# Sample states of the two recurrences in six half buffers instead of three whole ones

## The chip, the cores and the metric

The kernel runs on one core of one Trainium2 chip. The metric is device time in microseconds, from one launch of the whole program. Its engines are named as in the profile: PE is TensorE's matmul, PEld its weight load, DVE is VectorE, ACT is ScalarE, POOL is GpSimd, SP is SyncE; SPq is the queue on which SyncE issues DMAs.

## The reference, cut to what matters

The reference is one step of a hybrid decoder layer for a prompt (512 tokens) and eight samples (8 tokens each) that share all weights. The layer projects the input once, runs a Mamba-2 recurrence (SSD) and an mLSTM recurrence beside each other, projects back, and follows with cross attention and a SwiGLU block. Each sample brings a state for each recurrence, and the new states are outputs. For a group of samples the two recurrences compute:

```python
# SSD, per head: h is 64 x 128 (16 heads)
y_inter = einsum('btgn,bgjpn->btgjp', cc, h) * exp(cum)[..., None]
h_new = h * exp(cum[:, -1])[..., None, None] + einsum('bsgj,bsgjp,bsgn->bgjpn', to_end, xc, bc)
# mLSTM, per head: C is 128 x 256 (4 heads), n is 128
num = einsum('btsh,bshv->bthv', s, vc) + s_inter[..., None] * einsum('bthd,bhdv->bthv', qc, c_st)
c_new = scale[..., None, None] * c_st + einsum('bsh,bshd,bshv->bhdv', w_end, kc, vc)
```

So each sample's state is read once by a matmul (what the tokens see of the old state), scaled by a decay, increased by an outer product of the sample's own tokens, and stored.

## The kernel before, in words

Everything is computed in 32-bit floats. Large weights are split in a high and a low part, so that a projection is three matmuls per block (L201, L202, L203 for most, L772 to L774 for the values); these fill TensorE nearly all the time. The program's instructions are put in order ahead of time by a planner that simulates the engines: an instruction that stands earlier in the program has precedence as soon as its inputs are there by the planner's clock, and later ones fill the gaps. The result is one fixed order for each engine and for each DMA queue; on the chip every engine takes its list in that order and waits where an input is late.

The change is in two stages, both of which run among projection matmuls.

**SSD of the samples** (pool `ssds`, from L651). `xdts` (tokens times step size) and `xes` (`xdts` times the decay to the end) are tiles of 64 x 16 x 64. `stacks` (L637) builds from them, once for each half batch `hb`, the two operands of the update in a 96-row form (copies on ACT at L643, L644, L646, L648, differences on DVE at L645, L647). Then a loop over `b` from 0 to 3 handles two samples at a time, `4 * hb + b` for `hb` 0 and 1. Each sample's state is a tile `h0` of 128 x 16 x 64 (512 KB), which the profile calls h. In a step:

- L711 loads the two states on SyncE's queue.
- L715 reads them: four matmuls, one for each group of eight heads `g` and half batch `hb`, each with a stationary of 32 columns and 512 moving columns. They accumulate over the steps in four strips of 32 rows of one PSUM tile `psh` (ps_hs in the profile). The profile shows each of these 32-bit matmuls as two records. Their order is given by L712 and L713:

```python
        for g in range(2):
            for hb in (1, 0):
```

- L721 masks the sample's tokens (ACT), L722 multiplies the whole state by its decay (POOL), L725 computes the outer product of a head group (`ps_hu`), L726 adds it on DVE, and L728 stores the whole state after the second group.

`xdts`, `xes` and the states share one tag, `t4`, with three buffers: the first two hold `xdts` and `xes` until their readers are done, and a later load waits until the state that was in its buffer has been stored. `psh` holds one of the two PSUM buffers of its pool during the loop, so `ps_hu` has the other.

**mLSTM of the samples** (pool `mls`, from L870). For each half batch, four samples follow each other. Each state `c0` (128 x 4 x 258, 516 KB, c in the profile) is loaded by L909, read by four matmuls at L911, one for each head, into four strips of `psn` (ps_nh), updated head by head by L918 (`ps_cu`) and L919 (one DVE instruction for decay and sum), and stored by L921. Here too the tag is `t4` with three buffers, in a pool of its own.

Of the kernel before, what the change touches and what calls it, by code (L numbers as in the profile page):

```python
# [11 lines left out]
F32 = mybir.dt.float32  # L12
F32R = mybir.dt.float32r
BF16 = mybir.dt.bfloat16
AF = mybir.ActivationFunctionType
ALU = mybir.AluOpType
# [3 lines left out]
P = 128  # L20
T = 576
TP = 512
TS = 64
# [93 lines left out]
def build(nc, tc, ctx, I, O):  # L117
    V, A, G, S, TE = nc.vector, nc.scalar, nc.gpsimd, nc.sync, nc.tensor
    mm = TE.matmul
# [22 lines left out]
    def BP(name="b"):  # L142
        return pb.tile([P, 512], F32, name=name, tag="b")
# [140 lines left out]
    wend = ml.tile([P, 5, 16], F32, name="wend")  # L284
# [20 lines left out]
    for k in range(KT):  # L305
        if k % 2 == 0:
            c = slice(128 * k, 128 * k + 256)
            S.dma_start(raws[0][:, c], I["win"][1][:, c])
        S.dma_start(xraw[:, k, :], I["xT"][:, k, :])
        if k % 2 == 0:  # L310
# [4 lines left out]
                                     op0=ALU.mult, op1=ALU.subtract)  # L315
# [27 lines left out]
    stop = gemm(ps0[2][1], [(*w2, KT)], U, UL, 256, 320, 0, NSS)  # L343
# [12 lines left out]
    stop = gemm(ps0[3][0], [(*w3, KT)], U, UL, 0, 256)  # L356
# [19 lines left out]
    vts = ml.tile([P, 4, 258], F32, name="vts")  # L376
    ghalf = ml.tile([P, KT], F32, name="ghalf")
    V.tensor_scalar(ghalf, PAR("g_ml"), 0.5, None, op0=ALU.mult)
    stb = ExitStack()
# [257 lines left out]
    def stacks(pool, a, b, hb, nb=1):  # L637

        r, o = slice(32 * hb, 32 * hb + 32), slice(32 - 32 * hb, 64 - 32 * hb)
        l = slice(64, 96)  # L640
        sa_ = pool.tile([96, a.shape[-1]], F32R, name="sta", tag="sta", bufs=nb)
        sb_ = pool.tile([96, b.shape[-1]], F32R, name="stb", tag="stb", bufs=nb)
        A.copy(sa_[r, :], a[r, :])  # L643
        A.copy(sa_[o, :], a[r, :])  # L644
        V.tensor_tensor(sa_[l, :], a[r, :], sa_[r, :].bitcast(F32), op=ALU.subtract)  # L645
        A.copy(sb_[r, :], b[r, :])  # L646
        V.tensor_tensor(sb_[o, :], b[r, :], sb_[r, :].bitcast(F32), op=ALU.subtract)  # L647
        A.copy(sb_[l, :], b[r, :])  # L648
        return sa_, sb_

    st2 = ExitStack()  # L651
    sd = st2.enter_context(tc.tile_pool(name="ssds", bufs=1, side="right", reuse_waits="tile"))
    masks8 = C16("masks")[:TS, :].unsqueeze(1).to_broadcast([TS, 8, TS])
    xdts = sd.tile([TS, 16, 64], F32, name="xdts", tag="t4", bufs=3)
    xes = sd.tile([TS, 16, 64], F32, name="xes", tag="t4", bufs=3)
    btk = sd.tile([TS, 2, P], F32, name="btk")
    for g in range(2):
        ps = BP("ps_xts")
        for j in range(4):
            TE.transpose(ps[:TS, j * P:(j + 1) * P], xs[:, g * 4 + j, TP:T], ident)  # L660
        V.tensor_tensor(xdts[:, 8 * g:8 * g + 8, :], ps[:TS, :].rearrange("p (h k) -> p h k", h=8),
                        CT[:TS, 4, 32 + 8 * g:40 + 8 * g].unsqueeze(2).to_broadcast([TS, 8, 64]), op=ALU.mult)
    ps = BP("ps_bts")
    for g in range(2):
        TE.transpose(ps[:TS, g * P:(g + 1) * P], bc[:, g, TP:T], ident)
    A.copy(btk, ps[:TS, 0:256].rearrange("p (g k) -> p g k", g=2))
    G.tensor_tensor(xes, xdts, wend[:TS, 4, :].unsqueeze(2).to_broadcast([TS, 16, 64]), op=ALU.mult)

    cpad = sd.tile([P, 2, NB, 32], F32, name="cpad")
    G.memset(cpad, 0.0)  # L670
# [8 lines left out]
    for g in range(2):  # L679
        psb = BP("ps_ls")  # L680
        pb3 = psb.rearrange("p (h t) -> p h t", h=8)
        for h in range(8):
            mm(psb[:, h * TS:(h + 1) * TS], sel[:80, 8 * g + h:8 * g + h + 1].to_broadcast([80, P]), cumst[:, TP:T],
               start=h == 0, stop=h == 7, skip_group_check=True)
        A.activation(decs[:, 8 * g:8 * g + 8, :], pb3[:, :, 7:TS:8], AF.Exp)
        lm = sd.tile([TS, 8, TS], F32, name="lms", tag="ts", bufs=1)
        V.tensor_tensor(lm, pb3[:TS], CT[:TS, 4, 8 * g:8 * g + 8].unsqueeze(2).to_broadcast([TS, 8, TS]), op=ALU.subtract)
        G.tensor_tensor(lm, lm, masks8, op=ALU.add)
        A.activation(lm, lm, AF.Exp)
        pcb = BP("ps_cbs")  # L690
        mm(pcb[:TS, :TS], bc[:, g, TP:T], bc[:, 2 + g, TP:T], start=True, stop=True)
        V.tensor_tensor(lm, lm, pcb[:TS, :TS].unsqueeze(1).to_broadcast([TS, 8, TS]), op=ALU.mult)
        for h in range(8):
            k, j = h % 2, (8 * g + h) // 2
            mm(psi[64 * k:64 * k + 64, j * TS:(j + 1) * TS], xdts[:, 8 * g + h, :], lm[:, h, :], start=True, stop=True,
               skip_group_check=True)
    yds = sd.tile([P, 8, TS], F32, name="yds", tag="ts", bufs=1)
    G.tensor_tensor(yds, xs[:, :, TP:T], PAR("dskip").unsqueeze(2).to_broadcast([P, 8, TS]), op=ALU.mult)
# [5 lines left out]
    A.activation(ecg[0:64, :], ps[0:64, 0:8], AF.Exp)  # L704
    A.activation(ecg[64:128, :], ps[64:128, 8:16], AF.Exp)
    psh = BP("ps_hs")
    hbs = [stacks(sd, btk.rearrange("p g k -> p (g k)"), xes.rearrange("p h k -> p (h k)"), hb, 2) for hb in range(2)]
    for b in range(4):
        hns = [sd.tile([P, 16, 64], F32, name="h0", tag="t4", bufs=3) for _ in range(2)]
        for hb in range(2):  # L710
            S.dma_start(hns[hb], I["h0"][4 * hb + b])  # L711
        for g in range(2):  # L712
            for hb in (1, 0):  # L713
                q = 32 * (2 * g + hb)
                mm(psh[q:q + 32, :], cpad[:, g, 4 * hb + b, :],  # L715
                   hns[hb][:, 8 * g:8 * g + 8, :].rearrange("p h k -> p (h k)"),
                   start=b == 0, stop=b == 3, skip_group_check=True)
        for hb in range(2):
            bb, hn, (bst, xst) = 4 * hb + b, hns[hb], hbs[hb]
            bm = sd.tile([96, 256], F32R, name="bm", tag="bm", bufs=1)  # L720
            A.activation(bm, bst.bitcast(F32), AF.Copy, scale=C32("bmask")[:96, b:b + 1])  # L721
            G.tensor_tensor(hn, hn, decs[:, :, bb:bb + 1].to_broadcast([P, 16, 64]), op=ALU.mult)  # L722
            for g in range(2):
                ps = BP("ps_hu")
                mm(ps, bm[:, g * P:(g + 1) * P], xst[:, g * 512:(g + 1) * 512], start=True, stop=True)  # L725
                V.tensor_tensor(hn[:, 8 * g:8 * g + 8, :], hn[:, 8 * g:8 * g + 8, :],  # L726
                                ps.rearrange("p (h k) -> p h k", h=8), op=ALU.add)
            S.dma_start(O["ssms"][bb], hn.rearrange("p h k -> p (h k)"))  # L728
    yin = sd.tile([P, 8, 64], F32, name="yin", tag="ts", bufs=1)
    V.tensor_tensor(yin, psh.rearrange("p (h k) -> p h k", h=8), ecg.unsqueeze(2).to_broadcast([P, 8, 64]), op=ALU.mult)  # L730
    ps = BP("ps_yt")
# [166 lines left out]
                    wendm[:TS, 4, :].unsqueeze(2).to_broadcast([TS, 4, P]), op=ALU.mult)  # L898
    for hb in range(2):
        r = slice(32 * hb, 32 * hb + 32)  # L900
        kst, vst = stacks(ms, kws.rearrange("p h k -> p (h k)"), vts.rearrange("p h k -> p (h k)"), hb)
        psn = BP("ps_nh")
        for h in range(4):
            mm(psn[32 * h:32 * h + 32, 0:257], ds_[r, h, r], vt[4][r, h, 0:257], start=True, stop=False,
               tile_position=(32 * hb, 32 * h), skip_group_check=True)
        for b in range(4):
            bb = 4 * hb + b
            c0 = ms.tile([P, 4, 258], F32, name="c0", tag="t4", bufs=3)
            S.dma_start(c0, I["c0"][bb])  # L909
            for h in range(4):  # L910
                mm(psn[32 * h:32 * h + 32, 0:257], qpad[:, h, bb, :], c0[:, h, 0:257], start=False, stop=b == 3,  # L911
                   skip_group_check=True)
            km = ms.tile([96, 512], F32R, name="km", tag="km", bufs=1)
            A.activation(km, kst.bitcast(F32), AF.Copy, scale=C32("bmask")[:96, b:b + 1])
            cn = c0
            for h in range(4):
                ps = BP("ps_cu")
                mm(ps[:, 0:258], km[:, h * P:(h + 1) * P], vst[:, h * 258:(h + 1) * 258], start=True, stop=True)  # L918
                V.scalar_tensor_tensor(cn[:, h, :], c0[:, h, :], es[:, h, 8 * bb + 7:8 * bb + 8], ps[:, 0:258],  # L919
                                       op0=ALU.mult, op1=ALU.add)  # L920
            S.dma_start(O["cs"][bb], cn)  # L921
        num = ms.tile([P, 1, 257], F32, name="nums", tag="nums", bufs=1)
        V.tensor_copy(num[:, 0, :], psn[:, 0:257])
        m4 = ms.tile([4, 4, 32], F32, name="m4t", tag="m4t", bufs=1)
        V.tensor_tensor(m4, C32("m4")[:4, :].rearrange("p (h t) -> p h t", h=4),
                        mrow[:, r].unsqueeze(1).to_broadcast([4, 4, 32]), op=ALU.mult)
        psx = BP("ps_mx")
        mm(psx[:, 0:1], m4.rearrange("p h t -> p (h t)"), ones[:4, :], start=True, stop=True)
        ex = ms.tile([P, 1], F32, name="exs", tag="exs", bufs=2)
        A.activation(ex, psx[:, 0:1], AF.Exp, scale=-1.0)  # L930
        f = head_norm(num, ex, 1, ms, "s")
        hn = ms.tile([P, 256], F32, name="hns", tag="hns", bufs=1)
        V.tensor_scalar(hn, num[:, 0, 0:256], f, None, op0=ALU.mult)
        pst = BP("ps_hts")
        for dv in range(2):
            TE.transpose(pst[:, dv * P:(dv + 1) * P], hn[:, dv * P:(dv + 1) * P], ident)
        A.copy(qk[:, :, TP + 32 * hb:TP + 32 * hb + 32], pst[:, 0:256].rearrange("p (d t) -> p d t", d=8))
# [1474 lines left out]
```

## Time and profile before

| what | value |
|---|---|
| median of the runs shown | 1121.05 us (1120.54 to 1121.95) |
| the profiled execution | 1117.7 us |
| its span, first to last instruction | 1115.9 us |
| mean granted TensorE clock over the span | 0.996 |
| PE busy | 1095.6 us (98%) |
| DVE, ACT, POOL busy | 771.4, 609.8, 223.5 us |
| matmuls L715 into psh | from 141.7 to 207 us |
| updates L726 of the SSD states | from 146.7 to 216.5 us |
| mLSTM states, first load to last store issued | from 260.5 to 390.2 us |

The profile is of one execution. In the rows of the timeline the first number is the start in us from the span's start, the second how long the row lasts, then come the engine, the line of the kernel, the operation, output<-inputs, the shape (for PE the stationary and then the moving operand) and how many records are merged into the row. A bracket at the end gives idle time of the engine just before, and what ended it. In a row of SPq the time is that of issuing the DMA, not of its transfer. In groups of instructions the columns are busy us and mean ns of one, then idle time before them. DMA issues give the size of one and the median us from issue to landing.

### The profile page before, as it was taken

How to read it: one execution, taken by the hardware profiler on the slowest of the kernel's cores; microseconds unless marked ns; L12 is line 12 of the kernel's file. 1: busy time of each engine (PE TensorE's matmuls, PEld its weight loads, DVE VectorE, ACT ScalarE, POOL GpSimd, SP SyncE). 2: the span in 40 equal slices, each digit the busy share in tenths (PEclk: the TensorE clock that was granted, in tenths of full speed). 3: DMA queues.
4: the chain of work that ended last, by engine and by line, in shares of the span. 5: the costliest groups of instructions: out<-in, count | busy, mean ns of one | idle time of the engine just before them, and what ended most of it. 6: DMA issues, size and time to landing. Idle time of an engine off the chain costs nothing.

```text
span 1115.9 us, 21276 instructions
## 1 busy us (share of the span) xinstructions
PE 1095.6 (98%) x8355; PEld 1043.4 (94%) x8355; DVE 771.4 (69%) x1521; ACT 609.8 (55%) x1130; POOL 223.5 (20%) x309
## 2 busy tenths in 40 slices
PE   9999999899999999999999999999999999999997
PEld 8999889798998999999988889999999999999997
DVE  6796875447786685568745455675578878887655
ACT  6877534246464365566534545644465556556654
POOL 1333544313113021110144401100000210020000
PEclk9999999999999999999999999999999999999999
DMA  6685565536464437973487755742552873397432
GB/s 210 159 165 130 132 180 144 172 71 163 128 204 111 118 101 260 294 279 96 151 268 263 254 204 163 229 158 88 169 157 82 188 170 88 83 234 219 103 138 85
DMA packets 60584, 184.44 MB, mean 165 GB/s; under 512 B 6684, under 2 KB 10908, under 8 KB 59972
## 3 DMA queue, kind: packets, MB, share of 16 engines
q1 hardware_dynamic: 44324, 142.19, 38.7%
q0 software_dynamic: 15872, 40.38, 17.5%
q8 instruction: 65, 1.06, 0.4%
q10 hardware_dynamic: 288, 0.52, 0.1%
q14 instruction: 35, 0.29, 0.1%
HBM read 153.75 MB, written 29.30 MB: 164 GB/s over the span
## 4 chain that ended last, share of the span: by engine, by line
PE 81%; DVE 6%; DMA 6%; ACT 5%; issue 2%; SPq 0%; DVEq 0%; ACTq 0%; POOLq 0%
PE ps_in L201 5%; PE ps_in L203 5%; PE ps_in L202 5%; PE ps_g L1725 3%; PE ps_g L1726 3%; PE ps_g L1727 3%; PE ps_u L1726 2%; PE ps_u L1725 2%; PE ps_u L1727 2%; PE ps_o L201 2%; PE ps_o L203 2%; PE ps_o L202 2%; PE ps_dn L201 2%; PE ps_dn L203 2%; PE ps_dn L1932 2%; PE ps_dn L202 2%
## 5 line engine op out<-in xcount | busy, mean ns | idle before, releaser
L201 PE MATMUL ps_in<-uh,whi 128*128 128x320 f32 (+1 forms) x544 | 165.9, 305 | 0.0
L203 PE MATMUL ps_in<-uh,wlo 128*128 128x320 f32 (+1 forms) x544 | 163.3, 301 | 0.1
L202 PE MATMUL ps_in<-ul,whi 128*128 128x320 f32 (+1 forms) x544 | 162.7, 299 | 0.0
L181 ACT CAST whi<-raw 128x1024 fp32r<-128x1024 f32 (+1 forms) x102 | 102.8, 1011 | 80.6 <-PE ps_in L202 19.5
L188 DVE TENSOR_TENSOR wlo<-raw,whi 128x512 fp32r<-128x512 f32 (+1 forms) x94 | 87.9, 935 | 62.4 <-ACT whi L181 61.8
L201 PEld LDWEIGHTS ps_in<-uh,whi 128*128 128x128 f32 x544 | 103.6, 190 | 2.6 <-issue 1.2
L203 PEld LDWEIGHTS ps_in<-uh,wlo 128*128 128x128 f32 x544 | 103.4, 190 | 2.0 <-issue 1.3
L202 PEld LDWEIGHTS ps_in<-ul,whi 128*128 128x128 f32 x544 | 103.6, 190 | 0.7
L186 POOL DMA_DIRECT2D wlo<-win x32 | 28.3, 886 | 94.5 <-ACT wlo L185 84.0
L1725 PE MATMUL ps_g<-b,whi 128*128 128x288 f32 x144 | 42.7, 297 | 1.2 <-ACT cc L1793 1.0
L1725 PE MATMUL ps_u<-b,whi 128*128 128x288 f32 x144 | 42.8, 298 | 0.0
L1726 PE MATMUL ps_u<-b,whi 128*128 128x288 f32 x144 | 42.5, 295 | 0.0
L1726 PE MATMUL ps_g<-b,whi 128*128 128x288 f32 x144 | 42.5, 295 | 0.0
L201 PE MATMUL ps_xo<-qh,whi 128*128 128x288 f32 x128 | 37.8, 300 | 1.0 <-ACT f_xo L1407 1.0
L201 PE MATMUL ps_o<-mixm_h,whi 128*128 128x256 f32 (+1 forms) x128 | 38.0, 297 | 0.3 <-ACT whi L181 0.3
L201 PE MATMUL ps_xq<-u2h,whi 128*128 128x320 f32 (+1 forms) x128 | 38.2, 303 | 0.0
L774 PE MATMUL ps_v<-wlo,uh 128*128 128x256 f32 x128 | 37.0, 293 | 1.1 <-DMA wlo<-wv 1.1
L202 PE MATMUL ps_xq<-u2l,whi 128*128 128x320 f32 (+1 forms) x128 | 38.0, 298 | 0.0
L203 PE MATMUL ps_xq<-u2h,wlo 128*128 128x320 f32 (+1 forms) x128 | 37.9, 297 | 0.0
L202 PE MATMUL ps_o<-mixm_l,whi 128*128 128x256 f32 (+1 forms) x128 | 37.9, 297 | 0.0
L203 PE MATMUL ps_xo<-qh,wlo 128*128 128x288 f32 x128 | 37.7, 296 | 0.0
L202 PE MATMUL ps_xo<-ql,whi 128*128 128x288 f32 x128 | 37.6, 295 | 0.0
(777 smaller groups left out, 3913.8 us busy)
## 6 DMA issues: line engine op xcount, KB each, us to landing
raw<-win SPq DMA_DIRECT2D x35, 512.0 KB, 3.8
raw<-wout SPq DMA_DIRECT2D x17, 512.0 KB, 4.2
kva<-kc SPq DMA_DIRECT2D x16, 512.0 KB, 6.5
kva<-vc SPq DMA_DIRECT2D x16, 512.0 KB, 6.4
raw<-wxq SPq DMA_DIRECT2D x13, 512.0 KB, 3.8
raw<-wgate SPq DMA_DIRECT2D x13, 512.0 KB, 5.3
raw<-wup SPq DMA_DIRECT2D x13, 512.0 KB, 3.5
wlo<-win POOLq DMA_DIRECT2D x24, 256.0 KB, 5.6
```

The source lines that it names most:

```text
L181: A.copy(hi[:, :n], raw[:, :n])
L186: G.dma_start(lo[:, a:b], src[:, a:b], accum_op=ALU.add)
L188: e.tensor_tensor(lo[:, a:b], raw[:, a:b], hi[:, a:b].bitcast(F32), op=ALU.subtract)
L201: mm(ps, wh, ah, start=i == 0, stop=False)
L202: mm(ps, wh, al, start=False, stop=False)
L203: m = mm(ps, wl, ah, start=False, stop=i == len(tiles) - 1)
L774: m = mm(o, ah, lo[:, j:j + 256], start=False, stop=k == KT - 1, skip_group_check=True)
L1725: mm(ps, wh, b[0][:, k, :], start=start and k == 0, stop=False, skip_group_check=True)
L1726: mm(ps, wh, b[1][:, k, :], start=False, stop=False, skip_group_check=True)
L1727: m = mm(ps, wl, b[0][:, k, :], start=False, stop=k == 3, skip_group_check=True)
L1932: mm(ps, wh, bl, start=False, stop=False, skip_group_check=True)
```

## The change

In the SSD stage `xdts`, `xes` and each state become pairs of tiles, one for each group of eight heads, all under one tag `half` with six buffers. Each half is loaded, read, multiplied by its decay, increased and stored by itself. The four matmuls into `psh` now follow each other by half batch and then by head group, each right behind its load in the program; the loop `for hb in (1, 0)` is gone. `stacks` takes its second operand as a list of parts and copies part by part. In the mLSTM stage a state becomes two tiles of two heads each under a tag `half` with six buffers; a half is stored after its second head. The number and the shapes of the matmuls stay, and so do the bytes moved and held.

```diff
+        w = b[0].shape[-1]
         sa_ = pool.tile([96, a.shape[-1]], F32R, name="sta", tag="sta", bufs=nb)
-        sb_ = pool.tile([96, b.shape[-1]], F32R, name="stb", tag="stb", bufs=nb)
+        sb_ = pool.tile([96, w * len(b)], F32R, name="stb", tag="stb", bufs=nb)
...
-        A.copy(sb_[r, :], b[r, :])
-        V.tensor_tensor(sb_[o, :], b[r, :], sb_[r, :].bitcast(F32), op=ALU.subtract)
-        A.copy(sb_[l, :], b[r, :])
+        for k, part in enumerate(b):
+            c = slice(k * w, (k + 1) * w)
+            A.copy(sb_[r, c], part[r, :])
+            V.tensor_tensor(sb_[o, c], part[r, :], sb_[r, c].bitcast(F32), op=ALU.subtract)
+            A.copy(sb_[l, c], part[r, :])
...
-    xdts = sd.tile([TS, 16, 64], F32, name="xdts", tag="t4", bufs=3)
-    xes = sd.tile([TS, 16, 64], F32, name="xes", tag="t4", bufs=3)
+    xdts, xes = [[sd.tile([TS, 8, 64], F32, name=k, tag="half", bufs=6) for _ in range(2)] for k in ("xdts", "xes")]
...
-    G.tensor_tensor(xes, xdts, wend[:TS, 4, :].unsqueeze(2).to_broadcast([TS, 16, 64]), op=ALU.mult)
+    for g in range(2):
+        G.tensor_tensor(xes[g], xdts[g], wend[:TS, 4, 8 * g:8 * g + 8].unsqueeze(2).to_broadcast([TS, 8, 64]), op=ALU.mult)
...
     for b in range(4):
-        hns = [sd.tile([P, 16, 64], F32, name="h0", tag="t4", bufs=3) for _ in range(2)]
+        hns = {}
         for hb in range(2):
-            S.dma_start(hns[hb], I["h0"][4 * hb + b])
-        for g in range(2):
-            for hb in (1, 0):
+            for g in range(2):
+                hns[hb, g] = hn = sd.tile([P, 8, 64], F32, name="h0", tag="half", bufs=6)
+                S.dma_start(hn, I["h0"][4 * hb + b][:, 8 * g:8 * g + 8, :])
                 q = 32 * (2 * g + hb)
-                mm(psh[q:q + 32, :], cpad[:, g, 4 * hb + b, :],
-                   hns[hb][:, 8 * g:8 * g + 8, :].rearrange("p h k -> p (h k)"),
+                mm(psh[q:q + 32, :], cpad[:, g, 4 * hb + b, :], hn.rearrange("p h k -> p (h k)"),
                    start=b == 0, stop=b == 3, skip_group_check=True)
         for hb in range(2):
...
-            G.tensor_tensor(hn, hn, decs[:, :, bb:bb + 1].to_broadcast([P, 16, 64]), op=ALU.mult)
             for g in range(2):
+                hn = hns[hb, g]
+                G.tensor_tensor(hn, hn, decs[:, 8 * g:8 * g + 8, bb:bb + 1].to_broadcast([P, 8, 64]), op=ALU.mult)
                 ps = BP("ps_hu")
                 mm(ps, bm[:, g * P:(g + 1) * P], xst[:, g * 512:(g + 1) * 512], start=True, stop=True)
-                V.tensor_tensor(hn[:, 8 * g:8 * g + 8, :], hn[:, 8 * g:8 * g + 8, :],
-                                ps.rearrange("p (h k) -> p h k", h=8), op=ALU.add)
-            S.dma_start(O["ssms"][bb], hn.rearrange("p h k -> p (h k)"))
+                V.tensor_tensor(hn, hn, ps.rearrange("p (h k) -> p h k", h=8), op=ALU.add)
+                S.dma_start(O["ssms"][bb][:, g * 512:(g + 1) * 512], hn.rearrange("p h k -> p (h k)"))
...
-            c0 = ms.tile([P, 4, 258], F32, name="c0", tag="t4", bufs=3)
-            S.dma_start(c0, I["c0"][bb])
+            c0 = []
+            for p in range(2):
+                c0.append(ms.tile([P, 2, 258], F32, name="c0", tag="half", bufs=6))
+                S.dma_start(c0[p], I["c0"][bb][:, 2 * p:2 * p + 2, :])
             for h in range(4):
-                mm(psn[32 * h:32 * h + 32, 0:257], qpad[:, h, bb, :], c0[:, h, 0:257], start=False, stop=b == 3,
+                mm(psn[32 * h:32 * h + 32, 0:257], qpad[:, h, bb, :], c0[h // 2][:, h % 2, 0:257], start=False, stop=b == 3,
                    skip_group_check=True)
...
-            S.dma_start(O["cs"][bb], cn)
+                V.scalar_tensor_tensor(cn, cn, es[:, h, 8 * bb + 7:8 * bb + 8], ps[:, 0:258], op0=ALU.mult, op1=ALU.add)
+                if h % 2:
+                    S.dma_start(O["cs"][bb][:, h - 1:h + 1, :], c0[h // 2])
```

More of the change, by code (lines that the diff above doesn't have):

```diff
@@ L660, in build @@
             TE.transpose(ps[:TS, j * P:(j + 1) * P], xs[:, g * 4 + j, TP:T], ident)
-        V.tensor_tensor(xdts[:, 8 * g:8 * g + 8, :], ps[:TS, :].rearrange("p (h k) -> p h k", h=8),
+        V.tensor_tensor(xdts[g], ps[:TS, :].rearrange("p (h k) -> p h k", h=8),
                         CT[:TS, 4, 32 + 8 * g:40 + 8 * g].unsqueeze(2).to_broadcast([TS, 8, 64]), op=ALU.mult)
@@ L694, in build @@
             k, j = h % 2, (8 * g + h) // 2
-            mm(psi[64 * k:64 * k + 64, j * TS:(j + 1) * TS], xdts[:, 8 * g + h, :], lm[:, h, :], start=True, stop=True,
+            mm(psi[64 * k:64 * k + 64, j * TS:(j + 1) * TS], xdts[g][:, h, :], lm[:, h, :], start=True, stop=True,
                skip_group_check=True)
@@ L706, in build @@
     psh = BP("ps_hs")
-    hbs = [stacks(sd, btk.rearrange("p g k -> p (g k)"), xes.rearrange("p h k -> p (h k)"), hb, 2) for hb in range(2)]
+    hbs = [stacks(sd, btk.rearrange("p g k -> p (g k)"), [t.rearrange("p h k -> p (h k)") for t in xes], hb, 2) for hb in range(2)]
     for b in range(4):
-        hns = [sd.tile([P, 16, 64], F32, name="h0", tag="t4", bufs=3) for _ in range(2)]
+        hns = {}
         for hb in range(2):
-            S.dma_start(hns[hb], I["h0"][4 * hb + b])
-        for g in range(2):
-            for hb in (1, 0):
+            for g in range(2):
+                hns[hb, g] = hn = sd.tile([P, 8, 64], F32, name="h0", tag="half", bufs=6)
+                S.dma_start(hn, I["h0"][4 * hb + b][:, 8 * g:8 * g + 8, :])
                 q = 32 * (2 * g + hb)
-                mm(psh[q:q + 32, :], cpad[:, g, 4 * hb + b, :],
-                   hns[hb][:, 8 * g:8 * g + 8, :].rearrange("p h k -> p (h k)"),
+                mm(psh[q:q + 32, :], cpad[:, g, 4 * hb + b, :], hn.rearrange("p h k -> p (h k)"),
                    start=b == 0, stop=b == 3, skip_group_check=True)
         for hb in range(2):
-            bb, hn, (bst, xst) = 4 * hb + b, hns[hb], hbs[hb]
+            bb, (bst, xst) = 4 * hb + b, hbs[hb]
             bm = sd.tile([96, 256], F32R, name="bm", tag="bm", bufs=1)
             A.activation(bm, bst.bitcast(F32), AF.Copy, scale=C32("bmask")[:96, b:b + 1])
-            G.tensor_tensor(hn, hn, decs[:, :, bb:bb + 1].to_broadcast([P, 16, 64]), op=ALU.mult)
             for g in range(2):
+                hn = hns[hb, g]
+                G.tensor_tensor(hn, hn, decs[:, 8 * g:8 * g + 8, bb:bb + 1].to_broadcast([P, 8, 64]), op=ALU.mult)
                 ps = BP("ps_hu")
                 mm(ps, bm[:, g * P:(g + 1) * P], xst[:, g * 512:(g + 1) * 512], start=True, stop=True)
-                V.tensor_tensor(hn[:, 8 * g:8 * g + 8, :], hn[:, 8 * g:8 * g + 8, :],
-                                ps.rearrange("p (h k) -> p h k", h=8), op=ALU.add)
-            S.dma_start(O["ssms"][bb], hn.rearrange("p h k -> p (h k)"))
+                V.tensor_tensor(hn, hn, ps.rearrange("p (h k) -> p h k", h=8), op=ALU.add)
+                S.dma_start(O["ssms"][bb][:, g * 512:(g + 1) * 512], hn.rearrange("p h k -> p (h k)"))
     yin = sd.tile([P, 8, 64], F32, name="yin", tag="ts", bufs=1)
@@ L900, in build @@
         r = slice(32 * hb, 32 * hb + 32)
-        kst, vst = stacks(ms, kws.rearrange("p h k -> p (h k)"), vts.rearrange("p h k -> p (h k)"), hb)
+        kst, vst = stacks(ms, kws.rearrange("p h k -> p (h k)"), [vts.rearrange("p h k -> p (h k)")], hb)
         psn = BP("ps_nh")
@@ L914, in build @@
             A.activation(km, kst.bitcast(F32), AF.Copy, scale=C32("bmask")[:96, b:b + 1])
-            cn = c0
             for h in range(4):
+                cn = c0[h // 2][:, h % 2, :]
                 ps = BP("ps_cu")
                 mm(ps[:, 0:258], km[:, h * P:(h + 1) * P], vst[:, h * 258:(h + 1) * 258], start=True, stop=True)
-                V.scalar_tensor_tensor(cn[:, h, :], c0[:, h, :], es[:, h, 8 * bb + 7:8 * bb + 8], ps[:, 0:258],
-                                       op0=ALU.mult, op1=ALU.add)
-            S.dma_start(O["cs"][bb], cn)
+                V.scalar_tensor_tensor(cn, cn, es[:, h, 8 * bb + 7:8 * bb + 8], ps[:, 0:258], op0=ALU.mult, op1=ALU.add)
+                if h % 2:
+                    S.dma_start(O["cs"][bb][:, h - 1:h + 1, :], c0[h // 2])
         num = ms.tile([P, 1, 257], F32, name="nums", tag="nums", bufs=1)
```

## The prediction

> **What bounds the kernel now.** I read the page first (busy time, then what TensorE waited for), then the order of TensorE and of SyncE's DMA queue around the two sample recurrences, then the granted clock behind the two waits found there.
>
> ```profile
> PE 1095.6 (98%) x8355; PEld 1043.4 (94%) x8355; DVE 771.4 (69%) x1521; ACT 609.8 (55%) x1130; POOL 223.5 (20%) x309
> ...
> PE ps_hs L715 <- DMA h<-h: 2.6, 1, 2.6
> PE ps_nh L911 <- DMA c<-c: 1.9, 1, 1.9
> ```
>
> TensorE is busy for 98% of the span: anything the change does counts only as far as it makes TensorE idle, slow, or longer at work. The two longest waits of TensorE are both for a state load that this change cuts in two (columns: total, times, longest). They are followed by a slower clock (columns of the stretches: length, busy time and count of PE, PEld, DVE, ACT, POOL, then granted clock, DMA share, GB/s):
>
> ```profile
> 202.40:205.00 2.60, 0.04 (x1) 0.00 (x0) 0.00 (x0) 0.00 (x0) 0.00 (x0) 0.98 0.82 306
> 205.00:208.60 3.60, 3.55 (x17) 1.89 (x18) 0.69 (x1) 0.00 (x0) 1.53 (x1) 0.54 0.15 60
> ...
> 360.06:361.93 1.87, 0.00 (x0) 0.00 (x0) 1.87 (x4) 1.71 (x4) 1.35 (x3) 1.00 0.86 247
> 361.93:365.30 3.37, 3.37 (x19) 2.56 (x20) 3.37 (x7) 0.51 (x2) 0.76 (x1) 0.50 0.79 198
> ```
>
> So the SSM wait costs 2.60 + 3.60 x (1 - 0.54) = 4.3 us, and the mLSTM wait 1.87 + 3.37 x (1 - 0.50) = 3.6 us: **7.8 us is all that finer transfers can win at these two places.**
>
> A rule to weigh here: the Trainium skill, "TensorE: Matmul & The Clock Gate" (Part 1), puts the clock down after an idle window of about 3.4 us. This trace does not agree in size: 2.60 and 1.87 us of idle were enough (0.54 and 0.50). Were only the idle times at stake, as the rule would have it for waits this short, the prize would be 4.5 us and my sum below would end 1.7 us higher.
>
> **The change, part by part.**
>
> *Order of the reading matmuls (the largest term).* Each step b has four matmuls into four 32-row strips of psh. Today L713 takes hb = 1 first, the half batch that is loaded last:
>
> ```profile
> 138.67 0.33 SPq L711 DMA_DIRECT2D h<-h  x1
> 154.62 0.33 SPq L711 DMA_DIRECT2D h<-h  x1
> ...
> 161.03 1.07 PE L715 MATMUL ps_hs<-h,cpad 128*32 128x512 f32 x8
> 162.03 0.39 PE L203 MATMUL ps_in<-uh,wlo 128*128 128x256 f32 x1
> 162.48 0.40 PE L725 MATMUL ps_hu<-stb,bm 96*128 96x512 f32 x1
> ```
>
> The load of 138.67 had long been there (a load takes 4.0 us, row below), yet its two matmuls came only at 161.03, after the load of 154.62: matmuls into psh keep the program's order, and the first one waits for the later half. So all four go out together (x8 records, two each) and take 162.03 - 161.03 = 1.00 us. After the change the order is hb0g0, hb0g1, hb1g0, hb1g1, each with a load of its own, so each may go as soon as its 256 KB are there, with projection matmuls between them. The price of that is in the mLSTM rows, where the planner has already parted a group:
>
> ```profile
> 300.54 0.63 PE L911 MATMUL ps_nh<-c,qpad 128*32 128x257 f32 x6
> 301.11 0.38 PE L918 MATMUL ps_cu<-stb,km 96*128 96x258 f32 x1
> 301.42 0.62 PE L911 MATMUL ps_nh<-c,qpad 128*32 128x257 f32 x2
> 301.97 0.38 PE L201 MATMUL ps_in<-uh,whi 128*128 128x256 f32 x1
> ```
>
> Three matmuls together hold TensorE for 301.11 - 300.54 = 0.57 us, one alone for 301.97 - 301.42 = 0.55. Strips run beside each other, and a parted one costs 0.55/0.57 of a group. For the 512 columns of psh: 0.97 x 1.00 = **0.97 us for every extra group.** Nothing hides this, since it is TensorE's own time.
>
> How many groups? The halves come free one by one, at the pace of the updates:
>
> ```profile
> 146.71 0.69 DVE L726 TENSOR_TENSOR h<-h,ps_hu 128x512 f32<-128x512 f32 x1 [0.38 <-POOL h L722]
> 150.68 0.68 DVE L726 TENSOR_TENSOR h<-h,ps_hu 128x512 f32<-128x512 f32 x1
> 154.82 0.69 DVE L726 TENSOR_TENSOR h<-h,ps_hu 128x512 f32<-128x512 f32 x1 [1.43 <-PE ps_hu L725]
> 158.74 0.68 DVE L726 TENSOR_TENSOR h<-h,ps_hu 128x512 f32<-128x512 f32 x1
> 167.01 0.68 DVE L726 TENSOR_TENSOR h<-h,ps_hu 128x512 f32<-128x512 f32 x1
> ```
>
> An update every 4 us or so means a store, a freed half and a landed load every 4 us, far more than the 1 us that a group lasts. Step 0 finds all four halves loaded before TensorE gets there (one group, as now: rows of the first rival). In step 1 the hb0 halves go into the freed xdts or xes halves and land together (one group), hb1's follow two stores (two groups). In steps 2 and 3 all eight follow stores 4 us apart (eight). That is 12 groups for 4: 8 x 0.97 = **+7.8 us**. Bounds: only one more group in each of steps 1 to 3, 3 x 0.97 = +2.9; all sixteen alone, 12 x 0.97 = +11.6. I take 7.8 because the pace row puts the landings well apart.
>
> *mLSTM reading.* The four head matmuls of a sample keep their order; heads 0 and 1 now wait for one load, 2 and 3 for another. Three samples of each half batch still sit in six halves ahead of time. Only the fourth follows a store: in half batch 0 it is in two groups already (rows above), in half batch 1 one group becomes two, **+0.55 us** (0 if it stays whole; 4 x 0.55 = 2.2 if more part).
>
> *The two waits.* Each stands behind a hand-over on SyncE's queue: a store, its landing, a load into the same buffer.
>
> ```profile
> 151.43 0.34 SPq L728 DMA_DIRECT2D o_ssms<-h  x1
> ...
> 191.37 0.34 SPq L728 DMA_DIRECT2D o_ssms<-h  x1
> 200.98 0.33 SPq L711 DMA_DIRECT2D h<-h  x1
> ...
> 352.95 0.34 SPq L921 DMA_DIRECT2D o_cs<-c  x1
> 358.32 0.34 SPq L909 DMA_DIRECT2D c<-c  x1
> ...
> h<-h SPq DMA_DIRECT2D x8, 512.0 KB, 4.0
> o_ssms<-h SPq DMA_DIRECT2D x8, 512.0 KB, 4.9
> o_ssmp<-hs SPq DMA_DIRECT2D x2, 256.0 KB, 5.5
> raw<-wdown SPq DMA_DIRECT2D x8, 256.0 KB, 3.7
> ```
>
> The first hand-over took 154.62 - 151.43 = 3.2 us and cost no wait; that of 191.37 took 9.6 and that of 352.95 took 5.4, and those two made TensorE wait; the projection matmuls behind the waiting one stand too, since TensorE takes them in order. Half the bytes do not halve this: transfers of 256 KB land in 3.7 and 5.5 us, those of 512 KB in 4.0 and 4.9. What does help is that the first half leaves one update (4 us) earlier; the last half does not. The order is made ahead of time, so where the planned landing moves forward too, the wait can stay. Bounds: both waits gone, -7.8; or two new ones of that size, +7.8, as there are now ten hand-overs behind psh instead of six (loads 7 to 16 of 16, against 3 to 8 of 8). I take half the prize, **-3.9 us**.
>
> *The same work in twice as many instructions.*
>
> ```profile
> L722 POOL TENSOR_TENSOR h<-h,decs 128x1024 f32<-128x1024 f32 x8 | 15.8, 1989 | 6.9 <-PE ps_hs L715 6.9
> L587 POOL TENSOR_TENSOR xe<-xdt,wend 128x512 f32<-128x512 f32 x8 | 9.2, 1145 | 0.5 <-DVE xdt L583 0.5
> ...
> L646 ACT CAST stb<-xes x2: 1049/1050/1050, 115.1 to 117.2; 32x1024 fp32r<-32x1024 f32 x2
> L643 ACT CAST sta<-kws x2: 617/617/617, 271.7 to 317.0; 32x512 fp32r<-32x512 f32 x2
> ```
>
> The decay multiplies: 16 x 1.145 - 15.8 = 2.5 us more of POOL over 70 us; xes in two adds some 0.4. The stacks: 8 x 0.617 - 4 x 1.05 = 0.7 us more of ACT. The cover is that POOL and ACT do not bound TensorE here (20% and 55% busy); without it these few us would be spread over 16 steps that each gain more from starting at the half. SyncE issues 32 more DMAs at 0.33 us = 10.6 us over 280 us of its queue. What stands behind them there are weight loads; a store that waits for its update now holds them for one half at a time, more often. I count all of it as 0, with 1 us either way: a late weight load would be a new TensorE wait, an earlier POOL-issued weight transfer one less.
>
> **The sum.** 7.8 + 0.55 - 3.9 = +4.4 us against the profiled execution's own 1117.7 us (span 1115.9 and 1.8 around it): 1122.1. The median of the runs shown is 1121.05, that is 3.35 above the profiled one, so I predict **1125.5 us**, 0.4% slower. Its own range, with three to ten extra groups and none or one of the waits gone, is 1122 to 1131.
>
> **The rivals.**
>
> *Groups stay whole and both waits go.* The planner fills TensorE from its own clock; where its plan has the halves of a step land close together, or where higher-ranked work keeps TensorE busy until all four are there (as in step 0), there is no parting. For it: the row of 141.68 below, four at once although the loads were far apart. Against it: the pace row, and the x6 and x2 parted at 300.54. Time: 1121.05 - 7.8 = 1113.3, and up to 1118.8 with some parting. Chance 0.29. This is the other side.
>
> ```profile
> 109.79 0.33 SPq L711 DMA_DIRECT2D h<-h  x1
> 121.15 0.33 SPq L711 DMA_DIRECT2D h<-h  x1
> ...
> 141.68 1.07 PE L715 MATMUL ps_hs<-h,cpad 128*32 128x512 f32 x8
> ```
>
> *Parting and waits cancel.* Both effects happen in full: 7.8 + 0.55 - 7.8 = +0.55, 1121.6. Chance 0.18. For it: the SSM loop gets rid of its pause between steps (158.74 to 167.01, 8.3 us instead of 4), as a half no longer waits for the other half batch's matmul, so that the late loads come some 4 us earlier with every step.
>
> *The waits multiply.* Two of the eight hand-overs that TensorE followed at once (six behind psh, one behind psn in each half batch) came late. With ten and some four, a quarter is 3.5 late ones instead of 2: one or two more at 3.9 us each. With one net more: 7.8 + 0.55 + 3.9 = +12.3, 1133.3. Chance 0.10. For it: 256 KB takes as long to land as 512. The Trainium skill, "DMA: Bandwidth & Descriptors" (Anatomy of one DMA), gives for the software queue a fixed part of about 2 us per transfer whatever its size, which speaks against halving; these rows, on SyncE's queue, show the same flatness.
>
> **How the numbers follow.** The forecast has 0.43, the rivals 0.29, 0.18 and 0.10. A difference under 0.2% (2.2 us) can't be told from none in this kernel. Slower: 0.43 and 0.10, less a little that falls within 0.2%: 0.52. Within: 0.19. Faster: 0.29. The range runs from the first rival's end, 1113, to 1132, short of the third's; about 0.07 is left out below and 0.1 above.
>
> **What would show it.** Right: the rows of psh appear as x2 or x4 at some twelve places with projection matmuls between them, each holding TensorE about 1 us, psh's busy time goes up by some 8 us, and its load waits shrink but do not all go. Wrong: psh still in four x8 rows, or a single x2 that holds TensorE far under 0.97 us (the step on strips falls); no wait behind h or c at all with the clock at 1.00 there (the halves were worth the whole 7.8); or new waits on other lines, which would mean that the new order elsewhere decides and not these two stages.

## The result, and the profile after

The changed kernel took 1126.13 us in the median (1120.37 to 1129.9, 13 runs), the kernel before 1120.54 us beside it (1115.74 to 1122.73, 13 runs). The ratio is **1.0046, interval 1.0027 to 1.0064**: slower, by 3 to 7 us. The prediction was 1125.5 us and slower.

From the page of the changed kernel, busy time of the engines, and from its list of TensorE's waits:

```profile
PE 1105.9 (98%) x8355; PEld 1045.5 (93%) x8355; DVE 767.4 (68%) x1523; ACT 610.5 (54%) x1134; POOL 225.6 (20%) x318
...
PE ps_o L201 <- ACT whi L181: 2.6, 2, 1.9
PE ps_nh L915 <- DMA c<-c: 1.6, 2, 1.0
...
PE ps_hs L718 <- DMA h<-h: 1.3, 2, 1.0
```

TensorE executes the same 8355 matmul records and is busy for 1105.9 us in place of 1095.6 (1104.0 and 1099.3 in a second pair of traces, which is among the experiments). The waits for h and c are shorter, 1.3 and 1.6 us for 2.6 and 1.9, now in two pieces each. (The matmuls of L715 and L911 are L718 and L915 in the changed file.)

The timeline of the changed kernel, TensorE, all rows of psh, three of them with the row behind:

```profile
143.60 1.07 PE L718 MATMUL ps_hs<-h,cpad 128*32 128x512 f32 x8
144.60 1.09 PE L617 MATMUL ps_yi<-lm,xdt 128*64 128x128 f32 x16
...
146.89 1.05 PE L718 MATMUL ps_hs<-h,cpad 128*32 128x512 f32 x4
147.87 0.39 PE L203 MATMUL ps_in<-uh,wlo 128*128 128x256 f32 x1
...
154.65 1.04 PE L718 MATMUL ps_hs<-h,cpad 128*32 128x512 f32 x2
155.62 0.38 PE L202 MATMUL ps_in<-ul,whi 128*128 128x256 f32 x1
...
161.11 1.04 PE L718 MATMUL ps_hs<-h,cpad 128*32 128x512 f32 x2
...
167.15 1.05 PE L718 MATMUL ps_hs<-h,cpad 128*32 128x512 f32 x2
...
170.65 1.04 PE L718 MATMUL ps_hs<-h,cpad 128*32 128x512 f32 x2
...
177.44 1.05 PE L718 MATMUL ps_hs<-h,cpad 128*32 128x512 f32 x2 [0.28 <-DMA h<-h]
...
182.91 1.04 PE L718 MATMUL ps_hs<-h,cpad 128*32 128x512 f32 x2 [1.04 <-DMA h<-h]
...
188.97 1.04 PE L718 MATMUL ps_hs<-h,cpad 128*32 128x512 f32 x2
...
192.23 1.04 PE L718 MATMUL ps_hs<-h,cpad 128*32 128x512 f32 x2
...
197.32 1.05 PE L718 MATMUL ps_hs<-h,cpad 128*32 128x512 f32 x2
...
201.68 1.05 PE L718 MATMUL ps_hs<-h,cpad 128*32 128x512 f32 x2
```

One x8, one x4 and ten x2: twelve groups where there were four. One group of a single matmul holds TensorE for 155.62 - 154.65 = 0.97 us, the group of four for 144.60 - 143.60 = 1.00.

The groups of instructions of the changed kernel, by line, for psh and the decay multiplies (columns: busy, mean ns of one, idle time before):

```profile
L726 POOL TENSOR_TENSOR h<-h,decs 128x512 f32<-128x512 f32 x16 | 17.8, 1123 | 28.9 <-PE ps_hs L718 22.1 <-DVE h L729 6.8
L718 PE MATMUL ps_hs<-h,cpad 128*32 128x512 f32 x32 | 12.6, 605 | 1.3 <-DMA h<-h 1.3
```

The same group before had 5.1 us, of which some 0.8 were the slow clock (at full clock, in a second trace, it has 4.3):

```profile
L715 PE MATMUL ps_hs<-h,cpad 128*32 128x512 f32 x32 | 5.1, 718 | 2.6 <-DMA h<-h 2.6
```

The granted clock of the changed kernel around its longer psh wait (length, then busy time by engine, granted clock, DMA share, GB/s):

```profile
182.90:187.00 4.10, 4.09 (x28) 3.25 (x29) 1.30 (x3) 0.59 (x3) 1.08 (x1) 1.00 0.25 83
```

It stays at 1.00, and so it does behind the other three waits for h and c: the shorter waits cost their own length and no slow clock behind them.

**Where the profiled time went.** The two profiled spans are 11.8 us apart (1127.7 and 1115.9), twice the difference of the medians. The first SSM matmuls of the samples (ps_xts) begin at 102.6 before and 104.6 after, ahead of anything that the change touches. From there to the first matmul of the output projection (ps_o) is 405.8 - 102.6 = 303.2 us before and 411.4 - 104.6 = 306.8 after: **3.6 us more in the stretch that holds both stages.** The output projection up to the query projection (ps_xq) takes 522.2 - 405.8 = 116.4 us before and 534.0 - 411.4 = 122.6 after; all that follows takes 593.7 us in both. Whether those 6 us belong to the change was open; a second trace of both kernels is among the experiments.

### The profile page after: what moved, and what is told of

It is laid out like the page before. It is cut to its first block, busy times and chain, and to the rows that moved or that the text cites. A ratio compares the mean times of both kernels' runs of the same rounds, so it can differ in the third digit from the quotient of the medians.

```text
span 1127.7 us, 21360 instructions
## 1 busy us (share of the span) xinstructions
PE 1105.9 (98%) x8355; PEld 1045.5 (93%) x8355; DVE 767.4 (68%) x1523; ACT 610.5 (54%) x1134; POOL 225.6 (20%) x318
## 4 chain that ended last, share of the span: by engine, by line
PE 85%; DMA 6%; DVE 4%; ACT 3%; issue 1%; SPq 0%; DVEq 0%; ACTq 0%
PE ps_in L201 6%; PE ps_in L202 5%; PE ps_in L203 5%; PE ps_g L1729 3%; PE ps_g L1730 3%; PE ps_g L1731 3%; PE ps_u L1729 2%; PE ps_u L1730 2%; PE ps_u L1731 2%; PE ps_o L201 2%; PE ps_o L203 2%; PE ps_o L202 2%; PE ps_dn L201 2%; PE ps_v L776 2%; PE ps_v L775 2%; PE ps_v L774 2%
## 5 line engine op out<-in xcount | busy, mean ns | idle before, releaser
L203 PE MATMUL ps_o<-mixm_h,wlo 128*128 128x256 f32 (+1 forms) x128 | 38.8, 307 | 0.5 <-DVE wlo L188 0.5
L201 PE MATMUL ps_o<-mixs_h,whi 128*128 128x320 f32 (+1 forms) x128 | 38.2, 298 | 0.0
```

Source lines behind the costliest of these rows:

```text
L201: mm(ps, wh, ah, start=i == 0, stop=False)
L203: m = mm(ps, wl, ah, start=False, stop=i == len(tiles) - 1)
```

## The experiments

The table sums them up. "Groups" and "busy" are of psh, "waits" are TensorE's for h and for c, and "stretch" runs from the first matmul of ps_xts to the first of ps_o. The runs were made in several batches; each ratio is against runs of the kernel before in the same batch, so a quotient of two ratios can compare across batches and is rougher than either.

| kernel | groups, busy us | psn busy us | waits h, c us | stretch us | ratio (interval) |
|---|---|---|---|---|---|
| before | 4, 5.1 | 6.2 | 2.6, 1.9 | 303.2 | 1 |
| before, second trace | 4, 4.3 | 6.2 | 1.3, 2.6 | 301.2 | |
| after | 12, 12.6 | 5.9 | 1.3, 1.6 | 306.8 | 1.0046 (1.0027 to 1.0064) |
| after, second trace | 12, 12.6 | 5.9 | 0.7, 1.2 | 305.6 | |
| SSM last load first | 4, 4.3 | 6.3 | 1.6, 1.9 | 299.1 | 0.9983 (0.9963 to 1.0002) |
| mLSTM halves only | 4, 4.4 | 6.3 | 3.3, 2.2 | 302.8 | 0.9996 (0.9972 to 1.0020) |
| SSM halves only | 12, 12.6 | 5.9 | 2.3, 0.0 | 308.7 | 1.0080 (1.0057 to 1.0102) |
| whole, earlier load first | 7, 7.4 | 6.6 | 0.4, 0.0 | 300.5 | 1.0005 (0.9983 to 1.0027) |
| both last load first | 4, 4.3 | 5.3 | 1.8, 1.1 | 296.0 | 0.9978 (0.9957 to 0.9999) |
| SSM halves, last load first | 4, 4.3 | 6.0 | 1.4, 2.1 | 299.4 | 0.9975 (0.9955 to 0.9996) |

**Undo the order alone.** Loads, buffers, updates and stores stay in halves; only the four matmuls of a step are put behind all four loads, the last load's first.

```diff
                 S.dma_start(hn, I["h0"][4 * hb + b][:, 8 * g:8 * g + 8, :])
-                q = 32 * (2 * g + hb)
-                mm(psh[q:q + 32, :], cpad[:, g, 4 * hb + b, :], hn.rearrange("p h k -> p (h k)"),
-                   start=b == 0, stop=b == 3, skip_group_check=True)
+        for hb, g in ((1, 1), (1, 0), (0, 1), (0, 0)):
+            q = 32 * (2 * g + hb)
+            mm(psh[q:q + 32, :], cpad[:, g, 4 * hb + b, :], hns[hb, g].rearrange("p h k -> p (h k)"),
+               start=b == 0, stop=b == 3, skip_group_check=True)
```

> The kernel after, but in each SSM step all four half loads come first in the program and the four matmuls into psh follow in the order last load first (hb1g1, hb1g0, hb0g1, hb0g0). Loads, stores, updates and buffers stay in halves. Parting theory: psh is back to 4 groups of x8 records for 12, which takes 8 x 0.97 = 7.8 us off TensorE's busy time, so some 5 to 8 us under the kernel after, about 1118 to 1121 us, no slower than before. Rival (the loss comes from twice as many transfers and instructions, or from waits elsewhere): it stays within 2 us of the kernel after, 1124 to 1128 us.

Measured: 1117.28 us, ratio 0.9983 (0.9963 to 1.0002), a little under the 1118 to 1121 us of the parting theory. Its timeline, all rows of psh:

```profile
141.77 1.06 PE L719 MATMUL ps_hs<-h,cpad 128*32 128x512 f32 x8
...
159.47 1.06 PE L719 MATMUL ps_hs<-h,cpad 128*32 128x512 f32 x8
...
179.99 1.06 PE L719 MATMUL ps_hs<-h,cpad 128*32 128x512 f32 x8 [1.60 <-DMA h<-h]
...
196.13 1.06 PE L719 MATMUL ps_hs<-h,cpad 128*32 128x512 f32 x8
```

Four groups again, and the time is 0.9983/1.0046, some 0.6% or 7 us, under the kernel after. The transfers and instructions are as many as there. TensorE itself shows where the time was: the stretch of both stages in the second trace of the changed kernel, then in this one (length, then busy time by engine, granted clock, DMA share, GB/s):

```profile
102.70:408.30 305.60, 302.54 (x2272) 269.34 (x2269) 203.09 (x482) 143.92 (x281) 96.55 (x122) 1.00 0.52 141
...
102.80:401.90 299.10, 293.97 (x2271) 268.21 (x2269) 205.96 (x486) 143.43 (x281) 94.25 (x122) 1.00 0.53 142
```

At the same granted clock of 1.00 and with one record less, TensorE is busy for 302.54 - 293.97 = 8.6 us less, about eight groups, and idle for 2.1 us more (5.1 and 3.1). So the order of the reading matmuls made the loss, and the rival falls.

**One stage at a time.**

The first of two kernels takes from the change only what is in the mLSTM stage, so that against the kernel before it has these lines:

```diff
-            c0 = ms.tile([P, 4, 258], F32, name="c0", tag="t4", bufs=3)
-            S.dma_start(c0, I["c0"][bb])
+            c0 = []
+            for p in range(2):
+                c0.append(ms.tile([P, 2, 258], F32, name="c0", tag="half", bufs=6))
+                S.dma_start(c0[p], I["c0"][bb][:, 2 * p:2 * p + 2, :])
...
-            S.dma_start(O["cs"][bb], cn)
+                if h % 2:
+                    S.dma_start(O["cs"][bb][:, h - 1:h + 1, :], c0[h // 2])
```

> Only the mLSTM stage in halves, the SSM stage as before. Parting theory: psh stays in 4 groups of x8, psn gets one group more (+0.55 us), and the mLSTM wait of 3.6 us with its slow clock shrinks or stays: -3 to +1 us against before. Rival (doubled transfers cost time wherever they are): +2 us or more.

Measured: 1119.72 us, ratio 0.9996 (0.9972 to 1.0020). The mLSTM halves by themselves change nothing that can be told; the waits for h and c are of the old size (3.3 and 2.2 us).

The second takes only what is in the SSM stage:

```diff
-        hns = [sd.tile([P, 16, 64], F32, name="h0", tag="t4", bufs=3) for _ in range(2)]
+        hns = {}
         for hb in range(2):
-            S.dma_start(hns[hb], I["h0"][4 * hb + b])
...
+            for g in range(2):
+                hns[hb, g] = hn = sd.tile([P, 8, 64], F32, name="h0", tag="half", bufs=6)
+                S.dma_start(hn, I["h0"][4 * hb + b][:, 8 * g:8 * g + 8, :])
...
```

> Only the SSM stage in halves, the mLSTM stage as before. Parting theory: 12 groups, +7.8 us of TensorE time less up to 4.3 us for the SSM wait: +3.5 to +8 us against before, as much as the whole change. Rival (the mLSTM half makes the loss): within 2 us of before.

Measured: 1128.78 us, ratio 1.0080, +6 to +11 us. The SSM halves carry the whole loss, as the theory says. The size is over the +3.5 to +8 us that were expected: the stretch is 308.7 - 303.2 = 5.5 us longer than in the first trace of the kernel before, and the runs are 9 us slower by the ratio. That it loses more than the whole change is not shown, as the two intervals overlap (1.0057 to 1.0102 and 1.0027 to 1.0064). Its trace does have more idle time in the stretch than those of the changed kernel: it has no wait for c, but a longer one for h and one that neither of them has, right ahead of the first matmul of ps_o:

```profile
PE ps_hs L718 <- DMA h<-h: 2.3, 2, 1.7
PE ps_o L201 <- ACT mixs_h L192: 1.6, 1, 1.6
```

**The order without any halves.**

```diff
-            for hb in (1, 0):
+            for hb in (0, 1):
```

> The kernel before with whole buffers and one edit: the order of the half batches in front of the psh matmuls is (0, 1) in place of (1, 0), so that the first matmul of a step waits for the earlier load. No transfer and no instruction is added. Parting theory: steps 1 to 3 fall into two groups each, 7 groups for 4, 3 x 0.97 = +2.9 us of TensorE time, so +1 to +5 us against before. Rival (order is free, halves cost): within 1 us of before, with psh's busy time as before.

Measured: 1119.54 us, ratio 1.0005 (0.9983 to 1.0027), by the ratio 0.6 us over before. That is less than the +1 to +5 us of the parting theory; it is the rival's time, but not the rival's condition, for psh's busy time rose. The groups are as the parting theory had them (from the timeline of this kernel):

```profile
145.27 1.04 PE L715 MATMUL ps_hs<-h,cpad 128*32 128x512 f32 x2
146.25 0.39 PE L203 MATMUL ps_in<-uh,wlo 128*128 128x256 f32 x1
...
162.01 1.06 PE L715 MATMUL ps_hs<-h,cpad 128*32 128x512 f32 x6
163.00 0.50 PE L725 MATMUL ps_hu<-stb,bm 96*128 96x512 f32 x1
...
181.52 1.06 PE L715 MATMUL ps_hs<-h,cpad 128*32 128x512 f32 x6 [0.45 <-DMA h<-h]
```

An x2 at 145.27 holds TensorE for 0.98 us and the x6 of the same step, 17 us later, for another 0.99: each of the steps 1 to 3 is in two groups. psh's busy time is 7.4 us. With 4.3 for four groups and 12.6 for twelve, the three kernels lie on one line: 4.3 + 3 x 1.04 = 7.4 and 4.3 + 8 x 1.04 = 12.6. **The price of a group is shown**, without any half buffer in play. The net is not +2.9 us, since in this order the waits for h and c went from 2.6 and 1.9 us to 0.4 and none: over the whole stretch TensorE is idle for 2.3 us, in place of 6.8 and 6.2 in the two traces of the kernel before. So those waits are a matter of where the plan happens to put the matmuls; it does not take halves to lose them.

**Both stages last load first.**

```diff
-            for h in range(4):
+            for h in (3, 2, 1, 0):
                 mm(psn[32 * h:32 * h + 32, 0:257], qpad[:, h, bb, :], c0[h // 2][:, h % 2, 0:257], start=False, stop=b == 3,
```

(on top of the first experiment)

> As the run with the SSM matmuls last load first, and also in the mLSTM stage the heads in the order 3, 2, 1, 0, so that a sample's first matmul waits for its later half load. Parting theory: psh in 4 groups and each fourth sample's psn matmuls together, 2 x 0.55 = 1.1 us off TensorE against that run: about 0.2 to 0.4% under before. Rival (halves give nothing of their own, waits fall as they fall): within 0.2% of before.

Measured: 1117.66 us, ratio 0.9978 (0.9957 to 0.9999). psn's busy time falls from 6.3 to 5.3 us, about the 1.1 expected, and the stretch to 296.0 us, the shortest of all. Some 1 us of that is work moved elsewhere: TensorE executes 2264 records in this stretch for 2271 in the first experiment, and the output projection behind it takes 122.7 us for 119.5. In time the kernel cannot be told from the first experiment (0.9983), and its interval ends just under 1.

**The order alone, with only the SSM stage in halves.** The same four lines as in the first experiment, on top of the kernel with only SSM halves.

> Only the SSM stage in halves, its matmuls last load first; the mLSTM stage as before. Differs from the run with only the SSM stage in halves by the order of four matmuls alone. Parting theory: 8 groups less, 7.8 us under that run, so within 3 us of before. Rival (the SSM halves cost through transfers and instructions): still +5 us or more against before.

Measured: 1117.62 us, ratio 0.9975 (0.9955 to 0.9996). Against the kernel with only SSM halves that is 0.9975/1.0080, 1.0% or 11 to 12 us, for the order of four matmuls. The direction is the theory's; the size is above its 7.8, as that kernel's loss was above it too. In the stretch TensorE is busy for 294.7 us in place of 303.1, which is 8.5 us for eight groups.

**Second traces of both kernels.**

> The kernel before once more, for a second trace. If the waits of 2.6 and 1.9 us for the state loads belong to its order, they are there again with psh in 4 and the mLSTM groups as they were, and the stretch of the output projection, 116.4 us from its first matmul to that of the query projection in the first trace, moves by a few us from run to run; if the change had lengthened that stretch to 122.6 us by itself, this trace would again show about 116.

> The changed kernel once more, for a second trace. Parting theory: 12 groups again, the two stages again some 3 to 5 us longer than in the kernel before. If the 6 us more in the output projection of the first trace were that run's own, this trace has less there.

Measured: one run each, 1124.82 and 1125.73 us. The output projection up to ps_xq now takes 526.1 - 404.4 = 121.7 us in the kernel before and 529.8 - 408.3 = 121.5 in the changed one. So the 116.4 us of the first trace were that run's luck (the six other kernels have 119.5 to 122.7), and the 6 us are no part of the change. The two stages repeat: stretches of 301.2 and 305.6 us, 4.4 apart (3.6 in the first pair). The whole spans of this pair, 1123.0 and 1123.9 us, do not show it, since this execution of the kernel before was 596.9 - 594.1 = 2.8 us longer behind ps_xq, where the change touches nothing. From TensorE's waits of the second trace of the kernel before:

```profile
PE ps_o L201 <- ACT whi L181: 2.8, 2, 1.8
PE ps_nh L911 <- DMA c<-c: 2.6, 1, 2.6
PE ps_hs L715 <- DMA h<-h: 1.3, 1, 1.3
```

The wait in the output projection (2.8 us for a weight) is in the kernel before too. And the two state waits are there again, but with other lengths, 1.3 us behind h and 2.6 behind c.

## Why the prediction was right, point by point

- **Parting, the largest term: right in count and in price.** Twelve groups were foreseen, one in step 0, three in step 1, four each in steps 2 and 3; the trace has x8, then x4, x2, x2, then eight x2. One lone matmul of 512 columns was put at 0.97 us from rows of 257 columns, and took 0.97. Undoing the order alone took back 7 us.
- **mLSTM reading: +0.55 was too much.** In half batch 1 the fourth sample did part in two, as the changed kernel's timeline shows:

```profile
357.66 0.63 PE L915 MATMUL ps_nh<-c,qpad 128*32 128x257 f32 x4
...
367.50 0.63 PE L915 MATMUL ps_nh<-c,qpad 128*32 128x257 f32 x4 [0.98 <-DMA c<-c]
```

  But elsewhere groups moved together, and psn's busy time is 5.9 us for 6.2, where the latter holds some slow clock.
- **The two waits: half the prize was a fair guess with weak reasons.** In the first traces the waits kept 1.3 + 1.6 = 2.9 us of the 7.8, a gain of 4.9 where 3.9 was taken. In the second pair the prize was 1.3 + 2.6 and 1.7 of slow clock behind the latter, 5.6 us, and 0.7 + 1.2 = 1.9 were kept: a gain of 3.7. That 3.9 lies near both is partly luck, for the prize itself was that of one execution: in the second trace of the kernel before, the psh wait is 1.3 us and the matmuls behind it run at full clock (a row of its timeline, then one of its stretches):

```profile
203.84 1.07 PE L715 MATMUL ps_hs<-h,cpad 128*32 128x512 f32 x8 [1.26 <-DMA h<-h]
```

```profile
203.80:207.00 3.20, 3.16 (x24) 2.25 (x25) 0.69 (x1) 0.84 (x2) 2.00 (x2) 1.00 0.02 9
```

  And the step took halves for what removes waits, while another order of whole buffers removed more.
- **"Half the bytes do not halve this": right for c, not for h.** DMA issues of the changed kernel, size and median us to landing:

```profile
c<-c SPq DMA_DIRECT2D x16, 258.0 KB, 4.4
o_cs<-c SPq DMA_DIRECT2D x16, 258.0 KB, 3.3
h<-h SPq DMA_DIRECT2D x16, 256.0 KB, 2.8
o_ssms<-h SPq DMA_DIRECT2D x16, 256.0 KB, 3.7
```

  Whole loads and stores of h took 4.0 and 4.9 us in the first trace of the kernel before and 5.5 and 6.3 in the second; halves took 2.8 and 3.7, then 2.6 and 4.0. That is 1.2 us less in the first pair and more than 2 in the second, so the other 256 KB transfers from which the prediction read flatness were a poor guide. Those of c hardly moved: in the list of DMA issues of the kernel before a whole c is loaded in 4.9 us and stored in 2.6.

- **The same work in twice as many instructions: right.** POOL's decay multiplies took 17.8 us for 15.8 (2.5 more foreseen), ACT is busy 610.5 us for 609.8 (0.7 foreseen), and no engine but TensorE shows it in the time: with the order undone, the same doubled instructions are no slower than before.
- **The clock behind a wait: right in price, but not set by the wait's length.** 1.87 and 2.60 us of idle were each followed by 3.4 us at half the clock, 1.7 us lost; the 1.60 us at 179.99 in the first experiment were not:

```profile
179.90:184.00 4.10, 4.01 (x39) 2.74 (x40) 0.38 (x1) 0.16 (x1) 2.88 (x3) 1.00 0.42 144
```

  The Trainium skill, "TensorE: Matmul & The Clock Gate" (Part 1), has a window of about 3.4 us that runs freely; that the same idle need not have the same effect fits such a window, that less than 3.4 us of idle were enough does not. The last section has what the traces show of it.
- **The rivals.** Groups staying whole did not happen in the changed kernel; it is what the first experiment made of it, at 0.9983. This rival's 1113.3 us were not reached there, since its other half failed: waits of 1.6 and 1.9 us for h and c stayed. Parting and waits did not cancel, as waits of 2.9 and 1.9 us were left, although the sign named for it came: from the first matmul of ps_xts to the last group of psh it is 97.1 and 96.4 us in the changed kernel, for 102.5 and 100.6 before. The waits did not multiply: two behind psh in either trace, 1.3 and 0.7 us in all.
- **Two slips in the working.** With three extra groups and one wait gone, the range's own end would be 1121.05 + 2.9 + 0.55 - 3.9 = 1120.6, not 1122. And the loads behind a store are five in the kernel before, not six: load 3, at 138.67, comes ahead of the first store at 151.43. The forecast uses neither.

The sum, against the two pairs of traces: +4.4 us foreseen, +3.6 and +4.4 in the stretch of both stages, and 3 to 7 us by the runs. The mechanism of the loss was right, and so was its largest term. The terms for the mLSTM reading and for the waits were rough; their errors, some 0.5 us and up to 1.0 us, are no larger than what two executions of one kernel differ by.

## What to carry to other kernels

Matmuls that fill different column strips of TensorE cost one matmul's time together and one each when parted (here 1.00 us for four and 0.97 for one). Where a planner issues work as soon as its inputs land, finer loads part them, so the one whose input comes last must stand first in the program. The halves themselves came out some 0.2% faster here once their readers were kept together (0.9983, 0.9978 and 0.9975, with intervals that end at 1.0002, 0.9999 and 0.9996), at the edge of what these runs can tell. Count what finer pieces do to the engine that bounds the kernel before counting what they do to waits.

## What the runs showed of the hardware that was not expected

The slow clock comes in spells of 3.41 us, whatever the length of the wait. In the kernel with only mLSTM halves, TensorE idled 3.3 us at psh, longer than in the kernel before. Around the two waits of the kernel before, and then around this one, cut where the clock changes (columns as above):

```profile
201.49:204.90 3.41, 0.95 (x8) 0.70 (x6) 0.00 (x0) 0.00 (x0) 0.00 (x0) 1.00 0.68 227
204.90:208.31 3.41, 3.26 (x14) 1.60 (x15) 0.69 (x1) 0.00 (x0) 1.24 (x1) 0.50 0.20 80
...
358.50:361.92 3.42, 1.56 (x11) 1.16 (x10) 2.96 (x6) 3.27 (x8) 1.43 (x3) 1.00 0.65 180
361.92:365.33 3.41, 3.40 (x19) 2.59 (x20) 3.41 (x7) 0.51 (x2) 0.77 (x1) 0.50 0.80 199
365.33:368.74 3.41, 3.41 (x30) 3.41 (x30) 1.30 (x5) 1.05 (x2) 0.00 (x0) 1.00 0.04 7
```

```profile
202.85:206.26 3.41, 0.77 (x8) 0.16 (x8) 0.00 (x0) 0.00 (x0) 0.00 (x0) 1.00 0.83 286
206.26:209.67 3.41, 3.41 (x18) 3.01 (x15) 0.69 (x1) 0.84 (x2) 2.86 (x2) 0.50 0.00 0
209.67:213.08 3.41, 3.41 (x25) 2.83 (x25) 2.14 (x4) 0.82 (x2) 2.34 (x3) 1.00 0.00 0
```

All three spells are 3.41 us at 0.50, a price of 1.7 us each, for waits of 2.6, 1.9 and 3.3 us; the third starts 0.8 us behind the end of its wait. Their starts lie on a grid within an execution: the two of the kernel before are 361.92 - 204.90 = 157.02 us apart, 46 times 3.413, and in its second trace spells start at 360.47, 483.35 and 722.28, which are 36 and 70 times 3.413 apart. (Some spells, as that at 483.35, last two steps of this grid, 6.8 us.)

So the share of idle time in the 3.41 us step of the grid ahead of a spell seems to count, and not the length of the wait: it is 3.41 - 0.95 = 2.5, 1.9 and 2.6 us in the rows above. In the seven traces that have spells, by which the grid can be placed, every step at full clock with 1.7 us of idle or more is followed by one, none with 1.4 or less is, and of three steps between (1.46, 1.53 and 1.61 us) only the first is. A wait that straddles two steps is split between them, and where the grid lies differs from run to run: counted back, its first step begins 0.1 us behind the span's start in the first trace of the kernel before and 2.1 us in the second. No experiment moved a wait against the grid, so this is read from the traces and not tested.
